# Gate and up projections of all FFN tiles with tokens on partitions: the weights move 512 columns a matmul, and VectorE turns the products with 32x32 transposes

## The chip, the cores and the metric

The kernel runs on one core of one Trainium2 chip. The metric is the device time of one execution in microseconds. The profile was taken by the hardware profiler during one execution; its "span" runs from the first to the last instruction.

## The reference

One decoder layer on 256 tokens (S) of width D = 2048, everything in float32: a half-step SwiGLU FFN, a mixer (sliding-window attention beside a convolution module), and a second half-step SwiGLU FFN, each followed by a layer norm over a scaled residual. The part that matters here is the FFN, which occurs twice with its own weights (D_FF = 5632):

```
def swiglu_ffn(x, w_gate, w_up, w_down):
    h = jax.nn.silu(x @ w_gate) * (x @ w_up)
    return h @ w_down

x = layer_norm(ALPHA * x + 0.5 * swiglu_ffn(x, ...), ln_g, ln_b)
```

## The kernel before

**Three products for one.** Each float32 operand is split into a rounded part `hi` and a rest `lo` (type float32r), and a product is the sum of hi·hi, hi·lo and lo·hi, accumulated in PSUM. The activations are kept as `xcat[128, 16, 2, 256]`: feature k*128+p on partition p, the hi and the lo part side by side, 256 tokens each. The weights come from HBM by SyncE as float32 in sources of 1 MB (`raw`, four buffers), each cut in two chunks of 128x1024. `Steps.split` (line 110) makes of each chunk a `hi` tile (ScalarE, L125) and a `lo` tile (VectorE, L127; for a few chunks around the mixer GpSimd). A chunk is handed out by `take()` and given back by `release()`. There are RING = 6 tiles of each kind, and a chunk is split at the earliest when it lies less than LEAD = 5 chunks ahead of the last one taken, so the splitting runs about five chunks ahead of the matmuls and then waits for TensorE to give a tile back.

**Order of the work.** The order on each engine is the order in which the program is written. `st.step()` marks a place between two pieces of TensorE work: it writes out jobs that are due (`st.at(n, job)` means n steps later), up to two splits, and then the jobs marked "after".

**The FFN.** The 44 tiles of 128 hidden features are done in two parts, 24 and then 20 tiles. In each part the gate and up products fill `hh`/`hl` (the hi and lo part of h, hidden features on partitions, 256 tokens); then `tokens_by` multiplies them with w_down into `acc`, with the tokens on partitions: the stationary operand is a 128x128 piece of `hh`/`hl`, the moving one 512 columns of weights, six matmuls for each half of the tokens and chunk (`token_mm`, `mm3`, L390 to L392).

The first two tiles of part 0 of each FFN are done by `token_group`, which has the form of `tokens_by`: tokens stationary (pieces of `xcat`), weights moving, 512 columns (gate of two tiles, then up of two tiles), 8 chunks and 96 matmuls into two PSUM tiles `grp` of 128 tokens each. Their SwiGLU result `ht` has tokens on partitions and is turned by four TensorE transposes into `tph` (L498).

The other 42 pairs of tiles (22 tiles in part 0, 20 in part 1, in two FFNs, 84 tiles) have features on partitions: the weights are stationary and the activations move. For one tile, TensorE does 32 matmuls with a `hi` weight and the 512 columns of `xcat[:, k]` (hi and lo tokens, L518), then 32 with a `lo` weight and the 256 columns of the hi tokens (L527). The two halves of the result are added (`corr` on ScalarE L540, `both` on VectorE L541), then silu (L544), the product `hf` (L545), and its split into `hh` (L548) and `hl` (L549).

Around it: `begun()` is called after the first two tiles; in FFN 2 it queues the residual work on VectorE (`residuals`, L359, L363, L364: four chunks of six operations, one chunk every six steps). PSUM holds four tiles of the kind `grp`/`acc` (`psB`) and two of the kind `gu` (`psA`).

Of the kernel before, what the change touches and what calls it, by code (L numbers as in the profile page):

```python
# [25 lines left out]
JT0 = 2  # L26
# [161 lines left out]
def hybrid_layer(  # L188
    ctx: ExitStack, tc: tile.TileContext, xT, x, wt1, wu1, wd1, win, wout, wt2, wu2, wd2,
# [15 lines left out]
    def add_ffn(wt, wu, wd):  # L205
        sources.extend(wt[q] for q in range(4))
        for j0, j1 in ((0, JA), (JA, JT)):
            for j in range(max(j0, JT0), j1):
                sources.extend((wu[j, 0], wu[j, 1]))
            for c in range(NC_):  # L210
                sources.extend(wd[c, g] for g in range(j0 // 4, j1 // 4))

    add_ffn(wt1, wu1, wd1)
# [6 lines left out]
    add_ffn(wt2, wu2, wd2)  # L220
# [254 lines left out]
    def ffn(xc, tag, skew, begun, prepare, finish):  # L475
        with tc.tile_pool(name=f"ffn{tag}", bufs=2) as pool:
            for part, (j0, j1) in enumerate(((0, JA), (JA, JT))):
# [3 lines left out]
                if part == 0:  # L481

                    ps = token_group(xc, skew)
                    tp = psA.tile([P, 2, 512], F32, tag="gu", name="tph")
                    hts = []

                    def swiglu(ps=ps, hts=hts, pool=pool):
                        for b in range(2):
                            sl = pool.tile([P, S], F32, tag="sl", name="slt")
                            nc.scalar.activation(sl, ps[b][:, :S], AF.Silu)  # L490
                            ht = pool.tile([P, S], F32, tag="hf", name="ht")
                            nc.vector.tensor_tensor(out=ht, in0=sl, in1=ps[b][:, S:], op=ALU.mult)
                            hts.append(ht)

                    def turn(tp=tp, hts=hts, hh=hh, hl=hl):
                        for b in range(2):
                            for i in range(JT0):
                                nc.tensor.transpose(  # L498
                                    tp[:, i, b * P : (b + 1) * P], hts[b][:, i * P : (i + 1) * P], ident
                                )  # L500
                        nc.scalar.copy(hh[:, :JT0], tp[:, :, :S])
                        nc.vector.tensor_tensor(
                            out=hl[:, :JT0], in0=tp[:, :, :S], in1=hh[:, :JT0].bitcast(F32), op=ALU.subtract
                        )

                    swiglu()
                    st.at(2, turn)
                    begun()
                for j in range(JT0 if part == 0 else 0, n):
                    gu = psA.tile([P, 2, 512], F32, tag="gu", name="gu")  # L510

                    parts = []
                    for n4 in range(4):
                        m, h = divmod(n4, 2)
                        parts.append(st.take())
                        for q in range(8):
                            k = 8 * h + q
                            nc.tensor.matmul(  # L518
                                gu[:, m, :], parts[n4][0][:, q * P : (q + 1) * P],
                                xc[:, k].rearrange("p a n -> p (a n)"), start=k == 0, stop=False,  # L520
                            )
                        st.step(1.8)
                    for n4 in range(4):
                        m, h = divmod(n4, 2)
                        for q in range(8):
                            k = 8 * h + q
                            nc.tensor.matmul(  # L527
                                gu[:, m, S:], parts[n4][1][:, q * P : (q + 1) * P], xc[:, k, 0, :],
                                start=False, stop=k == KT - 1,
                            )  # L530
                        st.release()
                        if n4 == 1:
                            st.step(1.9)
                    corr = pool.tile([P, 2, S], F32, tag="corr", name="corr")
                    both = pool.tile([P, 2, S], F32, tag="both", name="both")
                    sl = pool.tile([P, S], F32, tag="sl", name="sl")
                    hf = pool.tile([P, S], F32, tag="hf", name="hf")

                    def gate(gu=gu, corr=corr, both=both, sl=sl):
                        nc.scalar.copy(corr, gu[:, :, S:])  # L540
                        nc.vector.tensor_tensor(out=both, in0=gu[:, :, :S], in1=corr, op=ALU.add)  # L541

                    def swish(both=both, sl=sl, hf=hf):
                        nc.scalar.activation(sl, both[:, 0], AF.Silu)  # L544
                        nc.vector.tensor_tensor(out=hf, in0=sl, in1=both[:, 1], op=ALU.mult)  # L545

                    def split(j=j, hf=hf, hh=hh, hl=hl):
# [317 lines left out]
def _layout(inputs):  # L865
# [6 lines left out]
    def cols(w, n):  # L872
        return w.reshape(KT, P, n, P).transpose(2, 1, 0, 3).reshape(n, P, KT * P)
# [6 lines left out]
    def up(g, u):  # L880
        return np.stack([cols(g, JT), cols(u, JT)], axis=1)
# [60 lines left out]
```

## Time and profile before

| | |
|---|---|
| median of 3 runs (lowest, highest) | 1770.45 us (1770.28, 1772.87) |
| the profiled execution: time, span | 1771.41 us, 1769.6 us |
| TensorE (PE) busy | 1738.7 us, 98% of the span |
| VectorE (DVE) busy | 1054.9 us, 60% |
| ScalarE (ACT) busy | 831.4 us, 47% |
| GpSimd (POOL) busy | 181.0 us, 10% |
| read from HBM | 332.86 MB, 189 GB/s over the span |
| matmuls | 9550 |

Busy time of an engine is the time in which at least one of its instructions runs. Matmuls overlap: the records of neighbours lie over each other, so the mean length of one record is longer than the distance from one start to the next. What a matmul costs in a stream is read from the distance of starts.

### The profile page before, as it was taken

How to read it: one execution, taken by the hardware profiler on the slowest of the kernel's cores; microseconds unless marked ns; L12 is line 12 of the kernel's file. 1: busy time of each engine (PE TensorE's matmuls, PEld its weight loads, DVE VectorE, ACT ScalarE, POOL GpSimd, SP SyncE). 2: the span in 40 equal slices, each digit the busy share in tenths (PEclk: the TensorE clock that was granted, in tenths of full speed). 3: DMA queues.
4: the chain of work that ended last, by engine and by line, in shares of the span. 5: the costliest groups of instructions: out<-in, count | busy, mean ns of one | idle time of the engine just before them, and what ended most of it. 6: DMA issues, size and time to landing. Idle time of an engine off the chain costs nothing.

```text
span 1769.6 us, 23510 instructions
## 1 busy us (share of the span) xinstructions
PE 1738.7 (98%) x9550; PEld 1505.6 (85%) x9550; DVE 1054.9 (60%) x1367; ACT 831.4 (47%) x1145; POOL 181.0 (10%) x101
## 2 busy tenths in 40 slices
PE   8999999999999999999999999999999999999997
PEld 6888888888888888789988878888888888888885
DVE  5555555544555555648999777655555455555556
ACT  5544444334444443476655364544443334444431
POOL 0000000000000000268884010000000000000000
PEclk9999999999999999999999999999999999999998
DMA  8655555554555555454544546655555545555751
GB/s 315 236 190 191 191 190 207 196 192 171 190 189 191 190 204 199 149 185 160 169 155 167 190 167 213 215 190 191 191 199 198 198 170 190 189 191 190 243 208 48
DMA packets 52092, 336.48 MB, mean 190 GB/s; under 512 B 6288, under 2 KB 6416, under 8 KB 13072
## 3 DMA queue, kind: packets, MB, share of 16 engines
q1 hardware_dynamic: 51984, 334.98, 53.8%
q8 instruction: 75, 1.23, 0.3%
q14 instruction: 33, 0.27, 0.0%
HBM read 332.86 MB, written 2.10 MB: 189 GB/s over the span
## 4 chain that ended last, share of the span: by engine, by line
PE 86%; DVE 10%; ACT 2%; issue 1%; DMA 1%; SPq 0%; DVEq 0%; ACTq 0%
PE gu L518 35%; PE gu L527 18%; PE acc L392 10%; PE acc L390 10%; PE acc L391 10%; DVE conv L684 5%; PE grp L392 1%; PE grp L391 1%; PE grp L390 1%; DVE z L331 1%; DMA raw<-in_wt 1%; DVE nm L726 0%; DVE se L729 0%; DVE mx L725 0%; ACT pr L749 0%
## 5 line engine op out<-in xcount | busy, mean ns | idle before, releaser
L127 DVE TENSOR_TENSOR lo<-raw,hi 128x1024 fp32r<-128x1024 f32 (+1 forms) x550 | 660.8, 1218 | 508.4 <-issue 284.9
L125 ACT CAST hi<-raw 128x1024 fp32r<-128x1024 f32 (+1 forms) x614 | 632.9, 1047 | 328.1 <-PE acc L392 313.6
L518 PE MATMUL gu<-xcat,hi 128*128 128x512 f32 x2688 | 625.7, 390 | 0.0
L518 PEld LDWEIGHTS gu<-xcat,hi 128*128 128x128 f32 x2688 | 499.4, 188 | 100.3
L527 PEld LDWEIGHTS gu<-xcat,lo 128*128 128x128 f32 x2688 | 333.6, 192 | 6.5
L527 PE MATMUL gu<-xcat,lo 128*128 128x256 f32 x2688 | 335.6, 283 | 0.0
L390 PE MATMUL acc<-hi,hh 128*128 128x512 f32 x704 | 274.1, 389 | 0.0
L391 PE MATMUL acc<-lo,hh 128*128 128x512 f32 x704 | 273.9, 389 | 0.0
L392 PE MATMUL acc<-hi,hl 128*128 128x512 f32 x704 | 273.9, 389 | 0.0
L540 ACT COPY corr<-gu 128x512 f32<-128x512 f32 x84 | 49.3, 586 | 439.0 <-PE gu L527 438.9
L127 POOL TENSOR_TENSOR lo<-raw,hi 128x1024 fp32r<-128x1024 f32 x64 | 153.6, 2421 | 808.6 <-ACT hi L125 805.6
L391 PEld LDWEIGHTS acc<-lo,hh 128*128 128x128 f32 x704 | 132.2, 188 | 27.4
L392 PEld LDWEIGHTS acc<-hi,hl 128*128 128x128 f32 x704 | 132.2, 188 | 27.4
L390 PEld LDWEIGHTS acc<-hi,hh 128*128 128x128 f32 x704 | 132.2, 188 | 27.0
L684 DVE SCALAR_TENSOR_TENSOR conv<-hc,cw_sb,conv 128x256 f32<-128x256 f32 x232 | 106.9, 486 | 8.7 <-ACT conv L680 4.0
L541 DVE TENSOR_TENSOR both<-gu,corr 128x512 f32<-128x512 f32 x84 | 58.1, 691 | 84.1 <-ACT corr L540 84.1
L390 PE MATMUL in_c<-xcat,hi 128*128 128x256 f32 x256 | 73.9, 289 | 0.0
L391 PE MATMUL in_c<-xcat,hi 128*128 128x256 f32 x256 | 72.4, 283 | 0.0
L392 PE MATMUL in_c<-xcat,lo 128*128 128x256 f32 x256 | 72.4, 283 | 0.0
L271 DVE SCALAR_TENSOR_TENSOR xt<-acc,xt 128x512 f32<-128x512 f32 x48 | 33.1, 690 | 50.6 <-PE acc L392 50.6
L390 PE MATMUL acc<-hi,mh 128*128 128x512 f32 x128 | 51.0, 398 | 1.5 <-DVE hc L693 1.5
L390 PEld LDWEIGHTS in_c<-xcat,hi 128*128 128x128 f32 x256 | 49.0, 191 | 2.2 <-issue 1.8
(121 smaller groups left out, 1115.9 us busy)
## 6 DMA issues: line engine op xcount, KB each, us to landing
raw<-in_wu SPq DMA_DIRECT2D x168, 1024.0 KB, 4.8
raw<-in_wd SPq DMA_DIRECT2D x88, 1024.0 KB, 4.8
raw<-in_win SPq DMA_DIRECT2D x26, 1024.0 KB, 4.8
raw<-in_wout SPq DMA_DIRECT2D x16, 1024.0 KB, 4.8
raw<-in_wt SPq DMA_DIRECT2D x4, 1024.0 KB, 4.8
raw<-in_wt SPq DMA_DIRECT2D x6, 512.0 KB, 6.9
xt<-in_x SPq DMA_DIRECT2D x2, 1024.0 KB, 7.6
rg<-in_rows SPq DMA_DIRECT2D x8, 256.0 KB, 5.0
```

The lines of the kernel that those rows point to most:

```text
L125: nc.scalar.copy(hi, raw)
L127: eng.tensor_tensor(out=lo, in0=raw, in1=hi.bitcast(F32), op=ALU.subtract)
L271: nc.vector.scalar_tensor_tensor(out=y, in0=ps, scalar=factor, in1=y, op0=ALU.mult, op1=ALU.add)
L331: nc.vector.tensor_scalar(out=z, in0=xt[:, b, c * 512 : (c + 1) * 512], scalar1=mv[:, 0:1], scalar2=r, op0=ALU.subtract, op1=ALU.mult,)
L390: nc.tensor.matmul(ps, s_hi, m_hi, start=start, stop=False)
L391: nc.tensor.matmul(ps, s_hi, m_lo, start=False, stop=False)
L392: nc.tensor.matmul(ps, s_lo, m_hi, start=False, stop=stop)
L518: nc.tensor.matmul(gu[:, m, :], parts[n4][0][:, q * P : (q + 1) * P], xc[:, k].rearrange("p a n -> p (a n)"), start=k == 0, stop=False,)
L527: nc.tensor.matmul(gu[:, m, S:], parts[n4][1][:, q * P : (q + 1) * P], xc[:, k, 0, :], start=False, stop=k == KT - 1,)
L540: nc.scalar.copy(corr, gu[:, :, S:])
L541: nc.vector.tensor_tensor(out=both, in0=gu[:, :, :S], in1=corr, op=ALU.add)
L684: nc.vector.scalar_tensor_tensor(out=acc if k < CK - 1 else cv[:, i], in0=hc[:, k : k + S], scalar=cw_sb[:, i, k : k + 1], in1=acc, op0=AL ...
```

## The change

All pairs of tiles are now done as the first one was: `token_group` with tokens stationary and 512 columns of weights moving, 96 matmuls a pair. The weights in HBM are laid out for it (the same bytes, four sources a pair). The product `ht` with tokens on partitions is no longer turned on TensorE. VectorE does it with 16 transposes a pair, each on 32 partitions and 2x2 blocks of 32x32; four are written at each of the four steps after the pair's SwiGLU. The split into `hh` and `hl` follows at the fifth step, for both tiles at once. The tiles `gu`, `corr` and `both` of the FFN are gone, and in FFN 2 the rows of the last layer norm have buffers of their own.

```
-                if part == 0:
-                    ps = token_group(xc, skew)
-                    ...
-                            for i in range(JT0):
-                                nc.tensor.transpose(
-                                    tp[:, i, b * P : (b + 1) * P], hts[b][:, i * P : (i + 1) * P], ident
-                                )
-                    ...
-                for j in range(JT0 if part == 0 else 0, n):
-                    gu = psA.tile([P, 2, 512], F32, tag="gu", name="gu")
-                    for n4 in range(4):
-                        ...
-                            nc.tensor.matmul(
-                                gu[:, m, :], parts[n4][0][:, q * P : (q + 1) * P],
-                                xc[:, k].rearrange("p a n -> p (a n)"), start=k == 0, stop=False,
-                            )
-                        st.step(1.8)
-                    for n4 in range(4):
-                        ...
-                            nc.tensor.matmul(
-                                gu[:, m, S:], parts[n4][1][:, q * P : (q + 1) * P], xc[:, k, 0, :],
-                                start=False, stop=k == KT - 1,
-                            )
-                    ...
-                    gate()
-                    st.at(1, swish, True)
-                    st.at(2, split, True)
+                for j in range(0, n, JG):
+                    first = part == 0 and j == 0
+                    ps = token_group(xc, skew if first else 0)
+                    ht = pool.tile([P, 2, JG * P], F32, tag="ht", name="ht")
+                    hf = pool.tile([P, JG, S], F32, tag="hf", name="hf")
+
+                    def swiglu(ps=ps, ht=ht):
+                        for b in range(2):
+                            sl = pool.tile([P, JG * P], F32, tag="sl", name="sl")
+                            nc.scalar.activation(sl, ps[b][:, : JG * P], AF.Silu)
+                            nc.vector.tensor_tensor(out=ht[:, b], in0=sl, in1=ps[b][:, JG * P :], op=ALU.mult)
+
+                    def turn(f, ht=ht, hf=hf):
+                        for t in range(4):
+                            src = ht[32 * t : 32 * t + 32].rearrange("p b (j f n) -> p f b j n", j=JG, n=32)
+                            dst = hf[32 * f : 32 * f + 32].rearrange("p j (b t n) -> p t b j n", b=2, n=32)
+                            nc.vector.transpose(dst[:, t], src[:, f])
+
+                    def split(j=j, hf=hf, hh=hh, hl=hl):
+                        js = slice(j, j + JG)
+                        nc.scalar.copy(hh[:, js], hf)
+                        nc.vector.tensor_tensor(out=hl[:, js], in0=hf, in1=hh[:, js].bitcast(F32), op=ALU.subtract)
+
+                    swiglu()
+                    for f in range(4):
+                        st.at(1 + f, lambda f=f, turn=turn: turn(f), True)
+                    st.at(5, split, True)
+                    if first:
+                        begun()
```

In FFN 1, TensorE right after the first pair (`grp0`, `grp1` are the PSUM tiles of the two halves of the tokens, `tph` takes the turned product). Before:

```order
L518 MATMUL gu_325<-xcat0_75,hi8_262 128x512 x8
L518 MATMUL gu_325<-xcat0_75,hi9_278 128x512 x8
L498 MATMUL tph_310<-ident_89,ht_313 128x128 x2
L498 MATMUL tph_310<-ident_89,ht_317 128x128 x2
L518 MATMUL gu_325<-xcat0_75,hi10_284 128x512 x8
L518 MATMUL gu_325<-xcat0_75,hi11_300 128x512 x8
L527 MATMUL gu_325<-xcat0_75,lo8_263 128x256 x8
```

The same place after the change (all line numbers of these functions are one lower):

```order
L389 MATMUL grp0_324<-hi8_262,xcat0_75 128x512
L390 MATMUL grp0_324<-lo8_263,xcat0_75 128x512
L391 MATMUL grp0_324<-hi8_262,xcat0_75 128x512
L389 MATMUL grp0_324<-hi8_262,xcat0_75 128x512
L390 MATMUL grp0_324<-lo8_263,xcat0_75 128x512
L391 MATMUL grp0_324<-hi8_262,xcat0_75 128x512
L389 MATMUL grp1_325<-hi8_262,xcat0_75 128x512
```

A chunk, hi and lo, is now used up in 12 matmuls before the next one is touched; four hi chunks were used ahead of the first lo chunk before.

VectorE in FFN 1 from the first pair's SwiGLU on, before (`lo` are the weight splits):

```order
L492 TENSOR_TENSOR ht_313<-slt_311,grp0_124 128x256
L492 TENSOR_TENSOR ht_317<-slt_315,grp1_125 128x256
L127 TENSOR_TENSOR lo13_335<-raw11_238,hi13_334 128x1024
L502 TENSOR_TENSOR hl0_123<-tph_310,hh0_122 128x512
L127 TENSOR_TENSOR lo14_387<-raw12_260,hi14_386 128x1024
L127 TENSOR_TENSOR lo15_391<-raw12_260,hi15_390 128x1024
L541 TENSOR_TENSOR both_413<-gu_325,corr_412 128x512
```

and after the change:

```order
L491 TENSOR_TENSOR ht_310<-sl_312,grp0_124 128x256
L491 TENSOR_TENSOR ht_310<-sl_315,grp1_125 128x256
L127 TENSOR_TENSOR lo13_339<-raw11_238,hi13_338 128x1024
L498 STREAM_TRANSPOSE hf_311<-ht_310 32x2x2x32 x4
L127 TENSOR_TENSOR lo14_361<-raw12_260,hi14_360 128x1024
L498 STREAM_TRANSPOSE hf_311<-ht_310 32x2x2x32 x4
L127 TENSOR_TENSOR lo15_381<-raw12_260,hi15_380 128x1024
L498 STREAM_TRANSPOSE hf_311<-ht_310 32x2x2x32 x4
```

One split and four transposes now alternate for four steps.

VectorE in FFN 2 after the change, at the second pair, where the first chunk of residual work (`xt`) lies too:

```order
L127 TENSOR_TENSOR lo_8777<-raw_8608,hi_8776 128x1024
L362 TENSOR_TENSOR xt<-xt,rg_0_8698 128x512
L498 STREAM_TRANSPOSE hf<-ht 32x2x2x32 x4
L127 TENSOR_TENSOR lo_8800<-raw_8650,hi_8799 128x1024
L363 TENSOR_TENSOR xt<-xt,rb_0_8700 128x512
L498 STREAM_TRANSPOSE hf<-ht 32x2x2x32 x4
L127 TENSOR_TENSOR lo_8821<-raw_8650,hi_8820 128x1024
```

Here a step holds a split, a residual operation and four transposes.

## Rows read from the trace of the kernel before

**Rows 1.** The page, parts 1 and 2: busy time of each engine, and the busy tenths and granted clock of TensorE in 40 slices of the span.

```profile
PE 1738.7 (98%) x9550; PEld 1505.6 (85%) x9550; DVE 1054.9 (60%) x1367; ACT 831.4 (47%) x1145; POOL 181.0 (10%) x101
PE   8999999999999999999999999999999999999997
PEclk9999999999999999999999999999999999999998
```

**Rows 2.** The page, part 4: shares of the chain that ended last, by engine and by line.

```profile
PE 86%; DVE 10%; ACT 2%; issue 1%; DMA 1%; SPq 0%; DVEq 0%; ACTq 0%
PE gu L518 35%; PE gu L527 18%; PE acc L392 10%; PE acc L390 10%; PE acc L391 10%; DVE conv L684 5%; PE grp L392 1%; PE grp L391 1%; PE grp L390 1%; DVE z L331 1%; DMA raw<-in_wt 1%; DVE nm L726 0%; DVE se L729 0%; DVE mx L725 0%; ACT pr L749 0%
```

**Rows 3.** Busy time in three stretches: gate/up of FFN 1, down of FFN 1, gate/up of FFN 2 at its start. Columns: from:to, length, then busy time and instructions of PE, PEld, DVE, ACT, POOL, the granted clock, the DMA share and GB/s.

```profile
43.45:276.82 233.37, 233.37 (x1345) 206.72 (x1345) 127.63 (x147) 110.86 (x149) 0.00 (x0) 1.00 0.56 199
285.00:410.00 125.00, 125.00 (x554) 103.52 (x553) 60.74 (x54) 49.26 (x47) 0.00 (x0) 1.00 0.56 195
...
1061.66:1283.00 221.34, 221.34 (x1274) 195.93 (x1274) 134.23 (x164) 104.38 (x144) 0.00 (x0) 1.00 0.57 200
```

**Rows 4.** TensorE in order of time in FFN 1, from the last nine matmuls of the first pair (`grp`) through two tiles of the old form. Columns: start, length of the run of records, engine, line, what, count.

```profile
29.66 0.39 PE L390 MATMUL grp<-hi,xcat 128*128 128x512 f32 x1
...
31.70 3.79 PE L518 MATMUL gu<-xcat,hi 128*128 128x512 f32 x16
35.33 0.60 PE L498 MATMUL tph<-ident,ht 128*128 128x128 f32 x4
35.68 3.93 PE L518 MATMUL gu<-xcat,hi 128*128 128x512 f32 x16
39.45 4.00 PE L527 MATMUL gu<-xcat,lo 128*128 128x256 f32 x32
43.29 7.44 PE L518 MATMUL gu<-xcat,hi 128*128 128x512 f32 x32
50.57 4.00 PE L527 MATMUL gu<-xcat,lo 128*128 128x256 f32 x32
54.40 5.86 PE L518 MATMUL gu<-xcat,hi 128*128 128x512 f32 x25
```

**Rows 5.** TensorE in order of time, the first matmul of each stretch: down of part 0 of FFN 1, gate/up of part 1, down of part 1, and the same of FFN 2 from its first old-form tile on.

```profile
276.67 0.40 PE L390 MATMUL acc<-hi,hh 128*128 128x512 f32 x1
...
407.25 1.29 PE L518 MATMUL gu<-xcat,hi 128*128 128x512 f32 x5
...
629.49 0.40 PE L390 MATMUL acc<-hi,hh 128*128 128x512 f32 x1
...
1049.92 3.79 PE L518 MATMUL gu<-xcat,hi 128*128 128x512 f32 x16
...
1294.88 0.40 PE L390 MATMUL acc<-hi,hh 128*128 128x512 f32 x1
...
1425.46 2.88 PE L518 MATMUL gu<-xcat,hi 128*128 128x512 f32 x12
...
1647.70 0.40 PE L390 MATMUL acc<-hi,hh 128*128 128x512 f32 x1
```

**Rows 6.** Groups of instructions by line and form on VectorE and ScalarE. Columns: line, engine, operation, out<-in, shape, count | busy us, mean ns of one | idle before.

```profile
L127 DVE TENSOR_TENSOR lo<-raw,hi 128x1024 fp32r<-128x1024 f32 x546 | 658.1, 1222 | 506.4 <-issue 284.9 <-ACT hi L125 220.0
L125 ACT CAST hi<-raw 128x1024 fp32r<-128x1024 f32 x610 | 630.4, 1050 | 325.9 <-PE acc L392 313.6 <-DMA raw<-in_wt 3.7 <-PE gu L518 3.0
...
L492 DVE TENSOR_TENSOR ht<-slt,grp 128x256 f32<-128x256 f32 x4 | 1.6, 418 | 1.0 <-ACT slt L490 1.0
L490 ACT ACTIVATE slt<-grp 128x256 f32<-128x256 f32 x4 | 1.4, 383 | 1.3 <-PE grp L392 1.3
...
L502 DVE TENSOR_TENSOR hl<-tph,hh 128x512 fp32r<-128x512 f32 x2 | 1.4, 688 | 2.1 <-ACT hh L501 2.1
...
L501 ACT CAST hh<-tph 128x512 fp32r<-128x512 f32 x2 | 1.2, 587 | 3.0 <-PE tph L498 3.0
```

**Rows 7.** VectorE in order of time at the start of FFN 2, where its operations follow each other without a gap (L359, L363 and L364 are residual work).

```profile
1073.50 0.54 DVE L359 TENSOR_SCALAR xt<-xt,par 128x512 f32<-128x512 f32 x1
...
1075.69 0.68 DVE L363 TENSOR_TENSOR xt<-xt,rg 128x512 f32<-128x512 f32 x1
1076.30 0.42 DVE L545 TENSOR_TENSOR hf<-sl,both 128x256 f32<-128x256 f32 x1
1076.63 1.22 DVE L127 TENSOR_TENSOR lo<-raw,hi 128x1024 fp32r<-128x1024 f32 x1
1077.77 0.68 DVE L364 TENSOR_TENSOR xt<-xt,rb 128x512 f32<-128x512 f32 x1
```

**Rows 8.** ScalarE in order of time in the down stretch of FFN 1: a split (`hi`) and, in brackets, its idle time before and who ended it.

```profile
301.37 1.05 ACT L125 CAST hi<-raw 128x1024 fp32r<-128x1024 f32 x1 [1.67 <-PE acc L392]
304.09 1.05 ACT L125 CAST hi<-raw 128x1024 fp32r<-128x1024 f32 x1 [1.67 <-PE acc L392]
```

**Rows 9.** Busy time in two stretches of 22 and 23 us at the start of FFN 2, columns as in Rows 3.

```profile
1083.00:1106.00 23.00, 23.00 (x137) 20.46 (x136) 17.78 (x24) 9.33 (x13) 0.00 (x0) 1.00 0.56 184
1106.00:1128.00 22.00, 22.00 (x128) 19.46 (x128) 17.96 (x23) 13.04 (x18) 0.00 (x0) 1.00 0.68 241
```

More of the change, by code (lines that the diff above doesn't have):

```diff
@@ L25 @@
 JA = 24
-JT0 = 2
+JG = 2
 NC_ = D // 512
@@ L188, in hybrid_layer @@
 def hybrid_layer(
-    ctx: ExitStack, tc: tile.TileContext, xT, x, wt1, wu1, wd1, win, wout, wt2, wu2, wd2,
+    ctx: ExitStack, tc: tile.TileContext, xT, x, wu1, wd1, win, wout, wu2, wd2,
     rows, ln_cols, b_in, b_tok, sinks, cw, cpar, out,
@@ L203, in hybrid_layer, with add_ffn @@
     sources = []
-    def add_ffn(wt, wu, wd):
-        sources.extend(wt[q] for q in range(4))
+    def add_ffn(wu, wd):
         for j0, j1 in ((0, JA), (JA, JT)):
-            for j in range(max(j0, JT0), j1):
-                sources.extend((wu[j, 0], wu[j, 1]))
+            for g in range(j0 // JG, j1 // JG):
+                sources.extend(wu[g, q] for q in range(4))
             for c in range(NC_):
                 sources.extend(wd[c, g] for g in range(j0 // 4, j1 // 4))
-    add_ffn(wt1, wu1, wd1)
+    add_ffn(wu1, wd1)
     first = 2 * len(sources)
@@ L219, in hybrid_layer @@
     second = 2 * len(sources)
-    add_ffn(wt2, wu2, wd2)
+    add_ffn(wu2, wd2)
     items = [("w", i) for i in range(len(sources))]
@@ L509, in ffn @@
-                for j in range(JT0 if part == 0 else 0, n):
-                    gu = psA.tile([P, 2, 512], F32, tag="gu", name="gu")
-                    parts = []
-                    for n4 in range(4):
[L514 to L517, printed above, removed]
-                            nc.tensor.matmul(
-                                gu[:, m, :], parts[n4][0][:, q * P : (q + 1) * P],
-                                xc[:, k].rearrange("p a n -> p (a n)"), start=k == 0, stop=False,
-                            )
-                        st.step(1.8)
-                    for n4 in range(4):
-                        m, h = divmod(n4, 2)
-                        for q in range(8):
-                            k = 8 * h + q
-                            nc.tensor.matmul(
-                                gu[:, m, S:], parts[n4][1][:, q * P : (q + 1) * P], xc[:, k, 0, :],
-                                start=False, stop=k == KT - 1,
[L530 to L547, printed above, removed]
-                        nc.scalar.copy(hh[:, j], hf)
-                        nc.vector.tensor_tensor(
-                            out=hl[:, j], in0=hf, in1=hh[:, j].bitcast(F32), op=ALU.subtract
-                        )
-                    gate()
-                    st.at(1, swish, True)
-                    st.at(2, split, True)
-                    st.step(1.9)
@@ L586, in prepare3 @@
         for c in range(NC_):
-            g = pool.tile([P, 512], F32, tag=("corr", "both")[c % 2], name=f"g3{c}")
+            g = pool.tile([P, 512], F32, tag="g3", name=f"g3{c}", bufs=NC_)
             nc.sync.dma_start(g, rows[5, c * 512 : (c + 1) * 512].partition_broadcast(P))
@@ L880, in up @@
     def up(g, u):
-        return np.stack([cols(g, JT), cols(u, JT)], axis=1)
-    def up_tok(g, u):
-        return rows_of(np.concatenate([g[:, : JT0 * P], u[:, : JT0 * P]], axis=1))[0]
+        both = [w.reshape(D, JT // JG, 1, JG * P) for w in (g, u)]
+        return rows_of(np.concatenate(both, axis=2).reshape(D, 2 * DFF))
     heads = np.stack([np.arange(NT), np.arange(NT) + NT], axis=1)
@@ L904, in _layout @@
         "x": x,
-        "wt1": up_tok(f["ffn1_w_gate"][0], f["ffn1_w_up"][0]),
         "wu1": up(f["ffn1_w_gate"][0], f["ffn1_w_up"][0]),
@@ L909, in _layout @@
         "wout": rows_of(w_out),
-        "wt2": up_tok(f["ffn2_w_gate"][0], f["ffn2_w_up"][0]),
         "wu2": up(f["ffn2_w_gate"][0], f["ffn2_w_up"][0]),
```

15 lines of the change are left out of this document (removed).

## The prediction

> **What bounds the kernel now.** I read the busy shares first, then the chain that ended last, then the two kinds of FFN stretch. TensorE is busy for 1738.7 of 1769.6 us, at the upper clock in nearly every slice [rows 1], and it holds 86% of the chain, 53% on the two gate/up lines alone [rows 2]. In the gate/up stretches its busy time equals the length of the stretch (233.37 of 233.37 us) at a granted clock of 1.00, while VectorE has 127.63 and ScalarE 110.86 us [rows 3]. Nothing is waited for there, so a saving must come from fewer or cheaper matmuls, and a loss can only come from an engine that begins to hold TensorE up. The splits of the weights are not that engine: in the down stretch ScalarE starts one every 2.72 us and stands idle for 1.67 us before it until TensorE gives a tile back [rows 8].
>
> **TensorE: what a pair of tiles costs.** Old form: a tile starts at 43.29 us, its lo matmuls at 50.57, the next tile at 54.40 [rows 4]. That is 7.28 us for 32 matmuls of 512 columns (227.5 ns each) and 3.83 us for 32 of 256 (119.7 ns), 11.11 us a tile, 22.22 a pair. Half the columns don't take half the time: the two points give 0.421 ns a column and 11.9 ns that each matmul pays whatever its width. New form: a pair has 96 matmuls of 512 columns instead of 64 + 64. The columns are the same (49,152); 32 matmuls fewer are paid for.
>
> The new form stands in the trace already. The down stretch from 276.67 to 407.25 us [rows 5] holds 4 x 12 x 12 = 576 such matmuls, 226.7 ns each. The last nine of the first pair, which have the very operands of the new form (`xcat` stationary, weights moving), take from 29.66 to 31.70 us, 2.04 us, again 226.7 ns [rows 4]. So a new pair costs 96 x 0.2267 = 21.76 us.
>
> What is replaced are the four stretches from the first old-form tile to the first down matmul [rows 4, 5]: 31.70 to 276.67 (244.97 us), 407.25 to 629.49 (222.24), 1049.92 to 1294.88 (244.96), 1425.46 to 1647.70 (222.24), together 934.41 us. They hold 42 pairs and also the four TensorE transposes of each first pair, which go away: the tiles with them take 31.70 to 43.29, 11.59 us against 11.11 [rows 4], so about 0.5 us each, 1.0 us in all. New: 42 x 21.76 = 913.9 us. The saving, if TensorE goes on without a gap, is **20.5 us**.
>
> A rule of the Trainium skill speaks against this price (TensorE: Matmul & The Clock Gate, Back-to-back issue gap): a matmul is said to cost its columns at 2.4 GHz plus a fixed 2.5 ns or so, which for 42 x 32 matmuls fewer would be an estimated saving of 3.4 us, and 1767 us in the end. The trace disagrees: 512 columns took 226.7 ns and 256 took 119.7, far above what that rule gives for either, and the distance between the two leaves 11.9 ns for the fixed part. I go by the rows.
>
> **VectorE: what it gets and what hides it.** A new pair brings eight splits, two products of 128x256, 16 transposes of 32 partitions x 128 elements, and one `hl` of 128x512. By the mean lengths [rows 6] that is 8 x 1.222 + 2 x 0.418 + 0.688 = 11.3 us without the transposes. Where operations follow each other without a gap, the next starts earlier: 1.14 us after a split, 0.33 after 128x256, 0.61 after 128x512 [rows 7], and the sum is 8 x 1.14 + 2 x 0.33 + 0.61 = 10.4 us. All of it lies beside 21.76 us of TensorE work.
>
> No row of this case shows a VectorE transpose, so I bound it. The nearest rows are the 128x256 and 128x512 operations. Halving 128x256 down along their difference gives 0.418 - 0.135 = 0.28 us by length and 0.33 - 0.14 = 0.19 us by distance of starts. Above: if a transpose had to take its elements in and put them out one after the other, it would have the price of 256 elements, 0.42 us. That a transpose is cheaper than 0.19 us is excluded, since it moves 128 elements a partition. I take 0.28, because four independent transposes follow each other but each also reads what a shortly earlier VectorE operation wrote. Then a pair needs 11.3 + 16 x 0.28 = 15.8 us of 21.76 (73%); by the lower bound 13.4, by the upper 18.0. All three fit, so I cost the transposes at nothing. The cover is gone at (21.76 - 11.3)/16 = 0.65 us a transpose by lengths, or (21.76 - 10.4)/16 = 0.71 by distances. The Trainium skill gives one price (VectorE: DVE Perf Modes, The three transpose paths): 311 ns for 128x128 in bf16 on VectorE. At that price, an estimate, a pair would need 16.3 us, which also fits; for float32 on 32 partitions no run here shows it yet.
>
> Within a pair the load is uneven: four steps of 2.72 us hold a split and four transposes (1.22 + 4 x 0.28 = 2.3 us, with 0.42 it is 2.9), the other four hold at most a split and the products or `hl`. What waits behind the transposes in VectorE's queue is the next `lo` chunk, and TensorE needs that one only about four chunks later: LEAD lets the splits run five chunks ahead, 13.6 us, less 2.3 us for the split itself. An excess of 4 x 0.2 us at the upper bound is swallowed.
>
> **The one place where VectorE has more to do** is the start of FFN 2, where the residual work comes on top. It has 17.78 of 23 and 17.96 of 22 us there now [rows 9]. Six operations of about 0.6 us [rows 7] in every six steps make 8 x 0.6 = 4.9 us in a pair of eight steps. With 0.28 a pair then needs 20.7 us of 21.76: it still fits. With 0.42 it needs 22.9, 1.1 us too much, for three pairs (24 steps of residual work), 3.4 us against a lead of some 11. Nothing again.
>
> **ScalarE** loses `corr` and half of its small operations; a pair has 8 x 1.05 + 2 x 0.383 + 0.587 = 9.8 us [rows 6]. The silu now waits for the last matmul of a half group at the head of its queue, but the split behind it waits for the same chunk to be given back anyway. `hh` waits for the last transposes, of the step before. **PSUM:** a group takes two of four tiles, the next group the other two, so `ht` has 21 us to read its tile. **The last pair of a part** is turned during the first five steps of the down stretch, 13.6 us; its rows of `hh` are the last in the first sweep, needed after 11 (part 1: 9) steps, 29.9 (24.5) us. **DMA:** bytes and buffers are the same, at a share of 0.56, and one chunk per 2.72 us is the rate of the down stretch, which does not wait. **Start and end:** the first pair is unchanged, and so is everything after the last down stretch.
>
> **Sum.** Made against the profiled execution: 1771.41 - 20.5 = 1750.9 us. That execution lay 1.0 us above the median of the runs; from the median, 1770.45 - 20.5 = **1750.0 us**.
>
> **Rivals.**
>
> *Transposes too dear (slower).* Place: VectorE in every pair. If one costs more than about 0.7 us, VectorE's period per pair passes TensorE's, each `lo` comes later than the one before, and once the lead of some 11 us is used up TensorE waits for VectorE. At 0.9 us the period is 10.4 + 14.4 = 24.8 us, 3.0 more than TensorE's, over 44 pairs 132 us, less up to 11 us of lead in each of four stretches: 1750 + 132 - 44, about 1840 us. It decides at 0.72 us: there the period is 21.9 and the gain still stands; about half a microsecond more a pair (0.75) gives the gain back. For: the operation is in no row. Against: it must cost 1.6 times my upper bound. Chance 0.07.
>
> *Columns are all that counts (no change).* The 11.9 ns might belong to the mix of 512 and 256 columns, not to each matmul; with the same columns a pair would then cost 22.2 us in either form, and only the 1.0 us of TensorE transposes is saved: 1769.5 us. The rule of the Trainium skill weighed above (TensorE: Matmul & The Clock Gate) would come out near this side, at 1767. Against: two stretches of the pure form, at 226.7 ns. Chance 0.05.
>
> *Local stalls (a smaller gain).* A transpose between 0.42 and 0.7 us leaves the steady pairs covered but not the start of FFN 2. At 0.6 us a pair there needs 11.3 + 9.6 + 4.9 = 25.8 us, 4.0 too much, 12 us over three pairs against a lead of 11; with it go late `hh` at a boundary or a bunched `raw`. That gives 1751 to 1762 us. Chance 0.11.
>
> *Forecast:* chance 0.77, between 1747 and 1753 us (a pitch between 226.2 and 227.5 ns is 2 us down and 3 us up).
>
> **The numbers.** Predicted 1750.0 us. The range goes from 1746 to 1760: the forecast's own range and most of the local stalls, 0.77 + 0.09, less a few hundredths for its edges; the two other rivals are left out. What this measurement can tell from no change is about 0.2%, 3.5 us. Faster by more than that: 0.77 + 0.11 = 0.88; the same: 0.05; slower: 0.07.
>
> **What would show it.** In the changed kernel the gate/up stretches should consist of `grp` matmuls at 226.7 ns from start to start and TensorE should stay busy for all of them; a pitch near 231 would mean that columns alone count. The mean of a transpose should lie between 0.19 and 0.42 us, VectorE's busy share in a gate/up stretch near 70%, and ScalarE should still wait for TensorE before its splits. If TensorE waits for `lo` from VectorE in `grp`, or ScalarE's `hh` waits for transposes for long, the cover is gone and the prediction is wrong; so it is if the granted clock falls in these stretches.

## The result, and the profile after

The changed kernel takes 1750.34 us (median of 4 runs, 1750.15 to 1750.41) against 1771.31 us of the kernel before, run beside it; the ratio is 0.9881, 95% interval 0.9864 to 0.9898, so 1.2% faster. The prediction was 1750.0 us. The profiled execution of the changed kernel took 1750.37 us with a span of 1748.6, so from profile to profile 21.0 us are gone, where the sum had said 20.5.

The page of the changed kernel, parts 1, 2 and 4 (to be read beside [rows 1, 2]):

```profile
PE 1716.8 (98%) x8198; PEld 1433.6 (82%) x8198; DVE 1220.8 (70%) x1945; ACT 804.4 (46%) x1019; POOL 181.1 (10%) x101
...
PEclk9999999999999999999999999999999999999998
...
PE 87%; DVE 10%; ACT 2%; issue 1%; DMA 0%; DVEq 0%; SPq 0%; ACTq 0%
PE grp L391 19%; PE grp L389 19%; PE grp L390 19%; PE acc L390 10%; PE acc L389 10%; PE acc L391 10%; DVE conv L638 5%; DVE z L330 1%; DVE nm L680 0%; DVE se L683 0%; DVE mx L679 0%; ACT pr L703 0%; ACT pr L689 0%; ACT L646 0%; DVE xt L270 0%
```

TensorE is still the bound (87% of the chain), with 1352 matmuls and 21.9 us of busy time fewer; the clock is where it was. The three lines of `grp` have taken the place of L518 and L527. VectorE went up by 165.9 us of busy time; its share of the chain is still 10%, and none of the lines named there is new work.

TensorE of the changed kernel in order of time, the first matmul of down and of gate/up around parts 0 and 1 of FFN 1 (as in [rows 5]):

```profile
270.37 0.39 PE L389 MATMUL acc<-hi,hh 128*128 128x512 f32 x1
...
400.93 0.39 PE L389 MATMUL grp<-hi,xcat 128*128 128x512 f32 x1
...
618.53 0.39 PE L389 MATMUL acc<-hi,hh 128*128 128x512 f32 x1
```

The same in FFN 2, from the second pair on:

```profile
1038.77 0.39 PE L389 MATMUL grp<-hi,xcat 128*128 128x512 f32 x1
...
1278.13 0.39 PE L389 MATMUL acc<-hi,hh 128*128 128x512 f32 x1
...
1408.69 0.39 PE L389 MATMUL grp<-hi,xcat 128*128 128x512 f32 x1
...
1626.29 0.39 PE L389 MATMUL acc<-hi,hh 128*128 128x512 f32 x1
```

The gate/up stretch of part 1 of FFN 1 is 400.93 to 618.53, 217.60 us for 10 x 96 matmuls: 226.7 ns each, 21.76 us a pair, the price that the prediction took from two stretches of before. It was 222.24 us long [rows 5]. FFN 2 shows the same 217.60 us for part 1, and 239.36 for the last 11 pairs of part 0.

Busy time in stretches of the changed kernel: three of 22 us at the start of FFN 2, and last one of a pair's length in FFN 1 (columns as in [rows 3]):

```profile
1072.00:1094.00 22.00, 22.00 (x99) 18.22 (x98) 20.46 (x37) 10.09 (x13) 0.00 (x0) 1.00 0.73 245
1094.00:1116.00 22.00, 22.00 (x99) 18.22 (x98) 18.63 (x31) 10.96 (x14) 0.00 (x0) 1.00 0.57 204
1116.00:1138.00 22.00, 22.00 (x98) 18.22 (x98) 21.46 (x41) 9.69 (x12) 0.00 (x0) 1.00 0.65 234
100.00:121.76 21.76, 21.76 (x98) 18.02 (x97) 15.91 (x28) 9.60 (x12) 0.00 (x0) 1.00 0.54 194
```

In a steady pair VectorE is busy for 15.91 of 21.76 us, and TensorE without a gap. At the start of FFN 2 VectorE comes up to 21.46 of 22 us, and TensorE still has no gap.

Groups of the changed kernel (line, engine, operation, shape, count | busy us, mean ns | idle before):

```profile
L125 ACT CAST hi<-raw 128x1024 fp32r<-128x1024 f32 x610 | 639.1, 1052 | 760.5 <-PE grp L391 343.1 <-PE acc L391 309.5 <-issue 100.6
...
L498 DVE STREAM_TRANSPOSE hf<-ht 32x128 f32<-32x128 f32 x704 | 212.8, 302 | 11.2
```

Four transposes in a row, by VectorE in order of time:

```profile
55.46 1.23 DVE L498 STREAM_TRANSPOSE hf<-ht 32x128 f32<-32x128 f32 x4
```

Its waits (who waited for whom: us in total, times, longest):

```profile
ACT hi L125 <- PE grp L391: 343.1, 212, 1.7
...
ACT rb L354 <- DMA rb<-in_rows: 17.5, 6, 4.1
...
ACT hh L502 <- DVE hf L498: 11.3, 4, 4.4
```

A transpose takes 302 ns, and four end 1.23 us after the first began, so they start 0.31 us apart and don't overlap. ScalarE's splits wait for TensorE in the gate/up stretches as they did in the down stretches [rows 8], so the splitting is ahead there. The exception is the start of FFN 2: there ScalarE stands at the head of its queue for a row of the residual (`rb`, up to 4.1 us) and for the transposes of a pair (`hh`, up to 4.4 us). TensorE has no gap beside either. The wait for `rb` is not new; the kernel before shows it at the same place, 5.25 us long:

```profile
1094.25 0.63 ACT L355 ACTIVATE rb<-rb 128x512 f32<-128x512 f32 x1 [5.25 <-DMA rb<-in_rows]
```

### The profile page after: what moved, and what is told of

It is laid out like the page before. It is cut to its first block, busy times and chain, and to the rows that moved or that the text cites. A ratio compares the mean times of both kernels' runs of the same rounds, so it can differ in the third digit from the quotient of the medians.

```text
span 1748.6 us, 21138 instructions
## 1 busy us (share of the span) xinstructions
PE 1716.8 (98%) x8198; PEld 1433.6 (82%) x8198; DVE 1220.8 (70%) x1945; ACT 804.4 (46%) x1019; POOL 181.1 (10%) x101
## 4 chain that ended last, share of the span: by engine, by line
PE 87%; DVE 10%; ACT 2%; issue 1%; DMA 0%; DVEq 0%; SPq 0%; ACTq 0%
PE grp L391 19%; PE grp L389 19%; PE grp L390 19%; PE acc L390 10%; PE acc L389 10%; PE acc L391 10%; DVE conv L638 5%; DVE z L330 1%; DVE nm L680 0%; DVE se L683 0%; DVE mx L679 0%; ACT pr L703 0%; ACT pr L689 0%; ACT L646 0%; DVE xt L270 0%
## 5 line engine op out<-in xcount | busy, mean ns | idle before, releaser
L125 ACT CAST hi<-raw 128x1024 fp32r<-128x1024 f32 (+1 forms) x614 | 641.5, 1049 | 762.2 <-PE grp L391 343.1
L127 DVE TENSOR_TENSOR lo<-raw,hi 128x1024 fp32r<-128x1024 f32 (+1 forms) x550 | 668.8, 1220 | 393.8 <-ACT hi L125 387.4
L389 PE MATMUL grp<-hi,xcat 128*128 128x512 f32 x1440 | 561.9, 390 | 5.9 <-ACT hi L125 5.9
L391 PE MATMUL grp<-hi,xcat 128*128 128x512 f32 x1440 | 561.6, 390 | 3.0 <-DVE xcat L317 3.0
L390 PE MATMUL grp<-lo,xcat 128*128 128x512 f32 x1440 | 561.5, 390 | 0.0
L389 PEld LDWEIGHTS grp<-hi,xcat 128*128 128x128 f32 x1440 | 271.0, 188 | 61.9 <-ACT hi L125 5.9
L391 PEld LDWEIGHTS grp<-hi,xcat 128*128 128x128 f32 x1440 | 270.8, 188 | 60.6 <-DVE xcat L317 4.3
L390 PEld LDWEIGHTS grp<-lo,xcat 128*128 128x128 f32 x1440 | 270.9, 188 | 57.2 <-DVE lo L127 0.8
L498 DVE STREAM_TRANSPOSE hf<-ht 32x128 f32<-32x128 f32 x704 | 212.8, 302 | 11.2
L490 ACT ACTIVATE sl<-grp 128x256 f32<-128x256 f32 x88 | 33.6, 384 | 52.1 <-PE grp L391 52.1
```

Source lines behind the costliest of these rows:

```text
L125: nc.scalar.copy(hi, raw)
L127: eng.tensor_tensor(out=lo, in0=raw, in1=hi.bitcast(F32), op=ALU.subtract)
L389: nc.tensor.matmul(ps, s_hi, m_hi, start=start, stop=False)
L390: nc.tensor.matmul(ps, s_hi, m_lo, start=False, stop=False)
L391: nc.tensor.matmul(ps, s_lo, m_hi, start=False, stop=stop)
L490: nc.scalar.activation(sl, ps[b][:, : JG * P], AF.Silu)
```

## The experiments

Times are compared with the changed kernel's 1750.34 us. Each experiment's ratio is against the kernel before, run beside it on the same chip (1771.7 to 1772.0 us there).

**Is it the number of matmuls?** The theory says that each matmul pays some 12 ns beside its columns; the rivals are that only columns count, or a fixed part of 2.5 ns. The first run makes the number of matmuls that of before, with the same columns. `narrow` is set for the gate/up pairs alone; the down matmuls stay as they are.

```
+            if narrow:
+                s_hi, s_lo = lhs[0][at], lhs[1][at]
+                nc.tensor.matmul(ps, s_hi, w[0][:, n], start=k == 0, stop=False)
+                for c in range(2):
+                    m = slice(q * 512 + c * 256, q * 512 + (c + 1) * 256)
+                    nc.tensor.matmul(ps[:, c * 256 : (c + 1) * 256], s_hi, w[1][:, m], start=False, stop=False)
+                nc.tensor.matmul(ps, s_lo, w[0][:, n], start=False, stop=k == nk - 1)
+                continue
             mm3(ps, lhs[0][at], lhs[1][at], w[0][:, n], w[1][:, n], k == 0, k == nk - 1)
```

> In all 44 gate/up pairs the hi-lo term is done as two matmuls of 256 columns instead of one of 512: 128 matmuls a pair, as before the change, with the same 49,152 columns. Theory (each matmul pays some 12 ns beside its columns): two halves at 119.7 ns are 239.4 against 226.7, 12.7 ns more, 44 x 32 x 12.7 ns = 17.9 us more than the changed kernel: 1768 us, the gain nearly gone. Rival (columns alone count, the gain came from something else in the change): 1750 us, no difference. By the fixed 2.5 ns of the Trainium skill (TensorE: Matmul & The Clock Gate, Back-to-back issue gap): 3.5 us more, 1754 us.

Measured: 1773.77 us, ratio 1.0007 (0.9998 to 1.0017), 23.4 us more than the changed kernel: the whole gain is gone. That is 23.4 us / 1408 = 16.6 ns for each matmul added, more than the 12.7 expected.

The second run halves nearly all of them:

```
+            if narrow:
+                for i, (s_, x_) in enumerate(((lhs[0][at], w[0]), (lhs[0][at], w[1]), (lhs[1][at], w[0]))):
+                    start, stop = k == 0 and i == 0, k == nk - 1 and i == 2
+                    cuts = [(0, 512)] if start or stop else [(0, 256), (256, 512)]
+                    for c0, c1 in cuts:
+                        nc.tensor.matmul(
+                            ps[:, c0:c1], s_, x_[:, q * 512 + c0 : q * 512 + c1], start=start, stop=stop
+                        )
+                continue
```

> As the run with one term in halves, but all three terms are in halves, except the first and the last matmul of each sum: 92 of 96 matmuls of a pair become two, 188 a pair. Theory: 44 x 92 x 12.7 ns = 51.4 us more than the changed kernel, 1802 us, slower than the kernel before; the price per matmul added is the same as with one term. Rival (columns alone): 1750 us. A second rival: the weight loads, 188 ns each, become the limit where all matmuls are short, and the price is more than 12.7 ns per matmul added: above 1802 us.

Measured: 1804.1 us, ratio 1.0181 (1.0166 to 1.0196), 53.8 us more: 53.8 us / 4048 = 13.3 ns for each matmul added, against 12.7. Both rivals with a smaller price are out (no difference; 2.5 ns, which would be 3.5 and 10 us). The rival that the weight loads become the limit has little left to explain: 0.6 ns for each matmul added.

Why did the first run pay 16.6 ns? TensorE of that run in order of time (L401 and L405 are the whole matmuls, L404 two halves):

```profile
99.95 0.39 PE L401 MATMUL grp<-hi,xcat 128*128 128x512 f32 x1
100.19 0.40 PE L404 MATMUL grp<-lo,xcat 128*128 128x256 f32 x2
100.42 0.40 PE L405 MATMUL grp<-hi,xcat 128*128 128x512 f32 x1
100.65 0.40 PE L401 MATMUL grp<-hi,xcat 128*128 128x512 f32 x1
100.89 0.39 PE L404 MATMUL grp<-lo,xcat 128*128 128x256 f32 x2
...
102.74 0.39 PE L401 MATMUL grp<-hi,xcat 128*128 128x512 f32 x1
```

From 99.95 to 102.74 there are four groups of two whole matmuls and two halves, 0.698 us each; three whole ones take 0.680. The two halves take some 0.23 us from start to start, no more than the 0.240 (226.7 + 13.3 ns) of two halves in the second run; the whole ones beside them take 0.23 to 0.24, where among themselves they take 0.227. So by the distances of starts the surplus lies with the 512-column matmuls next to narrow ones. What makes it was not tried.

**Does the change of the stationary operand matter?** Two of the three terms have the same one.

```
         nc.tensor.matmul(ps, s_hi, m_hi, start=start, stop=False)
-        nc.tensor.matmul(ps, s_hi, m_lo, start=False, stop=False)
-        nc.tensor.matmul(ps, s_lo, m_hi, start=False, stop=stop)
+        nc.tensor.matmul(ps, s_lo, m_hi, start=False, stop=False)
+        nc.tensor.matmul(ps, s_hi, m_lo, start=False, stop=stop)
```

> The three terms of a product stand in another order (hi-hi, lo-hi, hi-lo instead of hi-hi, hi-lo, lo-hi), so that the stationary operand changes with each matmul instead of staying for two of three. Theory (what a matmul pays beside its columns does not depend on that, since the weights are loaded for each matmul anyway): 1750 us, within 1 us. Rival (the distance of 226.7 ns is a mean over cheap matmuls with the same stationary operand and dear ones with a new one): more by at least 5 us, since one more change for each of about 2,100 triples of the FFNs at some nanoseconds each would show.

Measured: 1751.54 us (1750.65 to 1752.63), ratio 0.9882: 1.2 us more, just outside the 1 us of the theory, and not the 5 us of the rival. The edit also changes the matmuls of the mixer. Part 1 of FFN 1 in this run:

```profile
400.84 0.39 PE L389 MATMUL grp<-hi,xcat 128*128 128x512 f32 x1
...
618.44 0.39 PE L389 MATMUL acc<-hi,hh 128*128 128x512 f32 x1
```

It takes 217.60 us, as in the changed kernel, so in the FFN the order costs nothing. The distance of 226.7 ns is not a mean over cheap and dear matmuls.

**Are the transposes hidden, and would TensorE's have done?** First, without any:

```
-                    def split(j=j, hf=hf, hh=hh, hl=hl):
+                    def split(j=j, hf=ht, hh=hh, hl=hl):
...
                     swiglu()
-                    for f in range(4):
-                        st.at(1 + f, lambda f=f, turn=turn: turn(f), True)
                     st.at(5, split, True)
```

> The 704 VectorE transposes are left out, and hh and hl are made of the unturned product, so the result is not the layer's. Theory (VectorE's 213 us of transposes are hidden everywhere, at the start of FFN 2 too): 1750 us, within 1 us of the changed kernel, VectorE's busy time down by some 213 us. Rival (they hold TensorE up somewhere, at the start of FFN 2 or at the ends of the parts): 2 us or more below 1750.

Measured: 1750.58 us (1750.46 to 1750.66), ratio 0.9881. The page, part 1:

```profile
PE 1718.7 (98%) x8198; PEld 1435.2 (82%) x8198; DVE 1011.3 (58%) x1241; ACT 805.2 (46%) x1019; POOL 181.1 (10%) x101
```

VectorE has 209.5 us less to do, and the time is the same to 0.2 us. The transposes cost nothing, at the start of FFN 2 as elsewhere.

Then with the old way of turning, for all pairs:

```
+                    tp = psA.tile([P, 2, 512], F32, tag="gu", name="tph")
...
+                    def turn_pe(j=j, ht=ht, tp=tp, hh=hh, hl=hl):
+                        js = slice(j, j + JG)
+                        for b in range(2):
+                            for i in range(JG):
+                                nc.tensor.transpose(tp[:, i, b * P : (b + 1) * P], ht[:, b, i * P : (i + 1) * P], ident)
+                        nc.scalar.copy(hh[:, js], tp[:, :, :S])
...
-                    for f in range(4):
-                        st.at(1 + f, lambda f=f, turn=turn: turn(f), True)
-                    st.at(5, split, True)
+                    st.at(2, turn_pe)
```

> All pairs with tokens on partitions, but the products are turned by four TensorE transposes a pair, as the first pair was before the change, and not on VectorE. Theory: each pair's transposes cost TensorE what they cost in the kernel before, 0.48 us by the tiles 31.70 to 43.29 against 11.11 us (0.35 us by the starts alone): 44 x 0.35 to 0.48 = 15 to 21 us more than the changed kernel, 1766 to 1771 us, so without the VectorE transposes there would be little or no gain. Rival (TensorE has room for them): 1750 to 1753 us.

Measured: 1772.48 us, ratio 1.0004 (0.9995 to 1.0013), 22.1 us more than the changed kernel, 0.50 us a pair, a little above the 0.48 expected. TensorE of this run in order of time, around the transposes of one pair:

```profile
103.04 0.60 PE L497 MATMUL tph<-ident,ht 128*128 128x128 f32 x4
103.39 0.49 PE L389 MATMUL grp<-hi,xcat 128*128 128x512 f32 x1
103.71 0.39 PE L390 MATMUL grp<-lo,xcat 128*128 128x512 f32 x1
103.95 0.39 PE L391 MATMUL grp<-hi,xcat 128*128 128x512 f32 x1
```

The four transposes take 0.35 us, and the wide matmuls after them come 0.32 and 0.24 us apart instead of 0.227; that makes most of the 0.50. The tokens-on-partitions form alone gains nothing: what fewer matmuls save, TensorE's own transposes take back. The gain needs both parts of the change.

**How much room is left on VectorE?** All transposes twice, and in another run three times (`range(3)`):

```
-                            nc.vector.transpose(dst[:, t], src[:, f])
+                            for _ in range(2):
+                                nc.vector.transpose(dst[:, t], src[:, f])
```

> Every VectorE transpose is written twice (the second writes the same values again), 32 a pair. Theory (cover until VectorE's period reaches TensorE's 21.76 us): a pair needs 10.4 us by starts and 32 x 0.31 us of transposes, 20.3 us, so the steady pairs stay covered; at the start of FFN 2, with 4.9 us of residual work, it is 25.2, 3.4 us too much for three pairs, 10.3 us against a lead of some 11. So 1750 to 1754 us though 213 us of VectorE work are added. Rival (VectorE's lengths count and not its starts, or the lead is smaller): 11.3 + 32 x 0.302 = 21.0 us just fits, but 4 to 12 us appear at the start of FFN 2: 1755 to 1762 us.

Measured: 1764.53 us (1764.25 to 1765.89), ratio 0.9958: 14.2 us more, above both expectations. Busy time by stretch in that run (gate/up of FFN 1, then two stretches of FFN 2; columns as in [rows 3]):

```profile
15.00:270.00 255.00, 255.00 (x1126) 211.17 (x1125) 237.28 (x485) 117.87 (x136) 0.29 (x1) 1.00 0.59 218
...
1050.00:1130.00 80.00, 74.72 (x324) 59.94 (x323) 69.10 (x146) 29.80 (x38) 0.00 (x0) 1.00 0.53 184
1130.00:1275.00 145.00, 139.97 (x613) 114.54 (x612) 138.83 (x293) 59.74 (x74) 0.00 (x0) 1.00 0.53 190
```

In FFN 1 TensorE has no gap though VectorE is at 237 of 255 us; in FFN 2 it has gaps of 5.3 and 5.0 us. The gaps understate the loss, since a matmul that starts alone counts as busy for its whole record: the two stretches hold 324 and 613 matmuls, where the changed kernel's hold 355 and 642, and 60 matmuls at 226.7 ns are 13.6 us. Of VectorE's 80 us in the first of them 10.9 are idle. ScalarE and, below it, VectorE in order of time show why (in brackets the idle time before the instruction and who ended it):

```profile
1065.13 0.63 ACT L354 ACTIVATE rb<-rb 128x512 f32<-128x512 f32 x1 [6.25 <-DMA rb<-in_rows]
...
1086.63 0.62 ACT L503 CAST hh<-hf 128x512 fp32r<-128x512 f32 x1 [13.47 <-DVE hf L499]
...
1102.74 0.63 ACT L354 ACTIVATE rb<-rb 128x512 f32<-128x512 f32 x1 [8.73 <-DMA rb<-in_rows]
```

```profile
1066.74 1.23 DVE L127 TENSOR_TENSOR lo<-raw,hi 128x1024 fp32r<-128x1024 f32 x1 [6.28 <-ACT hi L125]
```

ScalarE stands 6.25 us at the head of its queue for a row `rb` that is still under way from HBM. The splits behind it do not start, and VectorE, which has too much to do, idles 6.28 us for want of a `hi`. Two more runs test whether this is the place, and whether this wait is the cause.

```
+                    def turn(f, ht=ht, hf=hf, times=1 if tag == "2" and part == 0 and j < 4 * JG else 2):
...
+                            for _ in range(times):
```

> As the run with every transpose twice, but the first four pairs of FFN 2, which run beside the residual work, have theirs once. Theory (that run's 14 us arise at the start of FFN 2 alone; the other 40 pairs are covered with twice the transposes): 1750 to 1752 us. Rival (a part of the 14 us lies in the steady pairs, where 21.2 of 21.76 us are used, or at the ends of the parts): 1755 to 1764 us.

Measured: 1750.77 us (1750.4 to 1755.28), ratio 0.9889. TensorE has no gap at the start of FFN 2 any more:

```profile
1050.00:1130.00 80.00, 80.00 (x355) 66.24 (x354) 67.78 (x117) 37.40 (x46) 0.00 (x0) 1.00 0.63 212
1130.00:1275.00 145.00, 145.00 (x642) 120.05 (x641) 137.18 (x296) 60.77 (x72) 0.00 (x0) 1.00 0.53 191
```

All 14 us arise from the first four pairs of FFN 2. The other run keeps every transpose twice and sets `tag2` for FFN 2:

```
-                    st.at(2 + n, x_, True)
+                    st.at((5 if tag2 else 2) + n, x_, True)
```

> As the run with every transpose twice, but in FFN 2 the residual operations, ScalarE's scaling of the row rb first, stand three steps later behind the issue of the transfers that they read. Theory A (ScalarE stood 6.3 and 8.7 us at the head of its queue for the row from HBM, the splits behind it came late, and VectorE had nothing to do meanwhile): most of the 14 us go, 1750 to 1757 us. Theory B (it is VectorE's load alone, 26 us a pair for three pairs against 21.76, and the wait for the row is a consequence): no change within 2 us, 1763 to 1766 us.

Measured: 1755.36 us (1755.28 to 1755.87), ratio 0.9907: 9.2 of the 14.2 us are gone. Busy time in the first stretch, and below it ScalarE at the same row:

```profile
1050.00:1130.00 80.00, 78.84 (x347) 64.61 (x345) 76.65 (x164) 30.78 (x40) 0.00 (x0) 1.00 0.57 197
```

```profile
1064.28 0.63 ACT L354 ACTIVATE rb<-rb 128x512 f32<-128x512 f32 x1
...
1103.74 0.62 ACT L503 CAST hh<-hf 128x512 fp32r<-128x512 f32 x1 [9.71 <-DVE hf L499]
...
1116.80 0.63 ACT L354 ACTIVATE rb<-rb 128x512 f32<-128x512 f32 x1 [3.73 <-DMA rb<-in_rows]
```

It does not wait there any more (of the four rows of FFN 2 only the last still does, 3.73 us), VectorE is busy for 76.65 us of the 80 instead of 69.10, and TensorE has gaps of 1.2 us. The load is the same, so load alone does not make the loss: about two thirds of it went when the residual work stood later. The edit moves VectorE's residual operations together with the row, so the run does not separate the wait for the row from the place of that work; the wait is the likelier cause, because VectorE's idle time in this stretch went with it, from 10.9 to 3.4 us. 5.0 us are left. Whether VectorE's load makes them or ScalarE's wait for `hh` (9.71 us in one place) was not tried.

> Every VectorE transpose is written three times, 48 a pair. Theory: 10.4 + 48 x 0.31 = 25.3 us a pair against 21.76, VectorE becomes the bound: 3.5 us x 44 pairs = 155 us, and 15 us for the residual work, less up to 11 us of lead in each of four stretches: some 1750 + 126 = 1876 us, between 1855 and 1900, with TensorE waiting for lo in the gate/up stretches. Rival (transposes of one pair run beside other VectorE work or are hidden by more than the lead): below 1850 us.

Measured: 1971.28 us, ratio 1.1123 (1.1107 to 1.114): 221 us more, above the expected 126. VectorE is the bound, as the theory had it, but two sizes were off. VectorE and ScalarE of this run in order of time, the `hl` of two neighbouring pairs and the first transposes of the last pair of part 0 of FFN 1, then the `hh` of the two pairs:

```profile
163.99 0.69 DVE L504 TENSOR_TENSOR hl<-hf,hh 128x512 fp32r<-128x512 f32 x1
...
190.62 0.69 DVE L504 TENSOR_TENSOR hl<-hf,hh 128x512 fp32r<-128x512 f32 x1
...
329.60 3.91 DVE L499 STREAM_TRANSPOSE hf<-ht 32x128 f32<-32x128 f32 x12
```

```profile
162.85 0.62 ACT L503 CAST hh<-hf 128x512 fp32r<-128x512 f32 x1 [14.40 <-DVE hf L499]
...
189.48 0.62 ACT L503 CAST hh<-hf 128x512 fp32r<-128x512 f32 x1 [15.99 <-DVE hf L499]
```

The period is 26.63 us, not 25.3: transposes in a row of 12 came 0.33 us apart. That gives (26.63 - 21.76) x 44 = 214 us, and with the 15 us taken for the residual work 229. By this estimate the lead gave back some 8 us in all, where four times 11 were expected. TensorE at the first down stretch shows where it went:

```profile
316.27 0.39 PE L389 MATMUL acc<-hi,hh 128*128 128x512 f32 x1
...
458.10 0.39 PE L389 MATMUL grp<-hi,xcat 128*128 128x512 f32 x1
```

This stretch begins 45.9 us later than in the changed kernel (270.37), which is 7.7 less than 11 x 4.87 us. But the stretch itself takes 141.83 us in place of 130.56, 11.3 more: VectorE comes into it late and begins to turn the last pair at 329.60, 13 us after TensorE began with down. What the lead covers in gate/up is paid in the down stretch. ScalarE stands for 14 to 16 us of each pair at `hh`, which waits for the last transpose, with the next splits behind it; it cannot work ahead while VectorE is late. The granted clock went down as well in this run, 0.95 on the mean over a gate/up stretch, so a part of it ran at the lower level of 1.2 GHz; TensorE was busy for 249 of its 280 us. Whether this cost time is not shown:

```profile
50.00:330.00 280.00, 248.69 (x1014) 197.00 (x1013) 263.52 (x613) 100.25 (x122) 0.00 (x0) 0.95 0.45 164
```

## Why the prediction was right

**The bound, right.** TensorE had no gap in the gate/up stretches before and has none after, from the second pair of each FFN on; the time there is the sum of the distances between matmuls.

**The price of a pair, right.** 96 matmuls at 226.7 ns, 21.76 us, measured 21.76. Only the cause was put a little too simply: "11.9 ns that each matmul pays whatever its width" came from two points, and the runs showed 13.3 ns per matmul added where nearly all were narrow and 16.6 where narrow and wide ones alternated. The change itself saved 0.46 us for 32 matmuls, 14.4 ns each; with 11.9 ns a pair would have come to 21.84 us, and the forecast was right because it took the 21.76 from a stretch of the same form. The Trainium skill (TensorE: Matmul & The Clock Gate, Back-to-back issue gap) gives the fixed 2.5 ns for a single matmul by itself, and 131 ns for 512 columns in a stream of weight loads and matmuls. Neither holds here: 512 columns take 226.7 ns in a stream, and both runs with halves stand against 2.5 ns.

**The sum, right.** 20.5 us were forecast for the four stretches, and they gave 5.6, 4.6, 5.6 and 4.6, 20.5 us. Another 0.5 us, up to the 21.0 from profile to profile, come from places that the sum put at nothing: the second pair of FFN 1 begins at 31.0 us (11 pairs of 21.76 before 270.37), where it began at 31.70 before [rows 4], 0.2 us are gone around the mixer, and the end is 0.4 longer. What makes these is not shown. That the median lies 0.3 us from the forecast is in part luck: the kernel before, beside which it was measured, took 0.9 us more than the 1770.45 from which the forecast was made, and that and the 0.5 us nearly cancel.

**VectorE in a steady pair, right.** 15.8 us of 21.76 were forecast, 15.91 measured. A transpose took 302 ns, against 280 taken and 190 to 420 as bounds; the price in the Trainium skill (VectorE: DVE Perf Modes, The three transpose paths), 311 ns for 128x128 in bf16, was near, though for another shape and type. The lower bound was too generous: 0.31 to 0.33 us from start to start, against 0.19. It took for granted that transposes overlap as the other operations do (1.14 us from start to start at 1.22 us of length [rows 6, 7]), and they don't. Leaving all transposes out changed nothing, so costing them at nothing was right.

**The start of FFN 2, right in its result, thin in its margin.** 20.7 us of 21.76 were forecast; stretches of 22 us show 20.46, 18.63 and 21.46. (8 x 0.6 is 4.8, not the 4.9 that the sum has; nothing hangs on it.) A sign that the prediction named for its being wrong, `hh` waiting for transposes for long, showed here a little: four waits, the longest 4.4 us, and they cost TensorE nothing. The wait for `rb`, in the trace before already, was in none of its terms.

**The lead, wrong in size, and without effect on the forecast.** The rivals' sums used "a lead of some 11 us" as if it could be spent whenever VectorE is late. Run with the transposes twice, 10 us of excess cost 14, and three times, four leads gave back 8 us in place of 44. Two things were left out. What waits behind the transposes is not `lo` alone: ScalarE's queue is coupled to them, since `hh` waits there for the last transpose, and `rb` for its transfer, each with the next `hi` splits behind it (moving the residual work away from its transfer gave 9.2 us back; for `hh` this is read from the trace and was not tried). And a lead is a delay: the down stretch behind pays for it. At the start of FFN 2 the changed kernel has room for 0.30 us a transpose and not for 0.6; the steady pairs had room for 0.6 too.

**The rivals.** Columns alone: refuted by two runs. Transposes too dear: forced by three transposes in place of one, 0.9 us, VectorE did become the bound, but the time was 1971 us, where this rival's sum gave 1840 for 0.9 us, with too short a period (24.8 for 26.63 us), without the residual work and with 44 us of lead. Local stalls: not in the changed kernel, but where they were placed, at the start of FFN 2, when the transposes were doubled; 1764.5 us came for 0.6 us a transpose, above its 1751 to 1762.

## What to carry to other kernels

Where TensorE is busy without a gap, read the distance of starts for each width: with the same columns, fewer and wider matmuls are cheaper, here by 13 to 17 ns for each matmul saved. A form that is cheaper on TensorE but needs its result turned pays only if another engine has the room for it; sum that engine's work over the period in the busiest stretch, not on average. And do not count a lead as saved: what it covers in one stretch was paid in the next one here. Look for instructions in the other queues that wait for the late work, or for a transfer, with the next splits behind them.

## What was not expected of the hardware

In these runs wide matmuls followed more slowly beside narrow ones. Beside 256-column matmuls a 512-column one came 0.23 to 0.24 us after the last start instead of 0.227, and after four TensorE transposes of 128 columns 0.32 and 0.24. The kernel before, which runs wide and narrow ones in blocks of 32, paid little of it: 7.28 us for 32 wide ones [rows 4], 227.5 ns each. What causes it stays open.
